# Pooled branch projection as three float32r products, and new rates for spreading the modulation sums

## The chip, the cores and the metric

One core of a Trainium2 chip runs the whole kernel in one launch. The metric is the device time in microseconds (us). The engines are PE (TensorE, matrix products), DVE (VectorE), ACT (ScalarE), POOL (GpSimd) and SP (which issues most DMA transfers). Each has a queue of its own and works through it in order; semaphores tie them together.

## The reference, cut to what matters

One decoder block for 256 tokens of width 2048, all in float32. The vector c gives six modulation rows (ada); the first half of the block mixes tokens by a sparse attention and by a causal pooling, merges both with gates and projects; the second half is a product-key retrieval over 16384 single-neuron experts, which the kernel computes densely.

```python
mod = einsum('bd,de->be', silu(c), w_ada) + b_ada            # 12288 values: sh1, sc1, gt1, sh2, sc2, gt2
h = rms_norm(x, g_norm1) * (1 + sc1) + sh1
q, k, v, iq, ik, iw, pl, ga, gp = split(h @ w_in)
attn = dsa_sparse_attention(...)                              # indexer scores, top 64 keys, softmax
pooled = trailing means of pl over 2/4/8/16 positions, minus pl
pooled = (per-group linear map of pooled) * pool_scale        # 256 tokens x 1024
y_pool = pooled @ w_pool_br                                   # 1024 -> 2048
merged = sigmoid(ga) * (attn @ w_attn_br) + sigmoid(gp) * y_pool
x = x + gt1 * (merged @ w_out)
h = rms_norm(x, g_norm2) * (1 + sc2) + sh2
x = x + gt2 * peer(h)                                         # q @ keys, top 16 x top 16, gelu(h @ u) * gates @ v
```

## The kernel before, in words

Activations lie with the features on the partitions: a tile is 128 features x 256 tokens, and 16 tiles make the width of 2048. Weights stream from HBM in rows of 128 x 2048 values (1 MB) into four buffers named `raw`, issued by SP in the order in which the program asks for them; a buffer is free for the transfer after next but three when its last reader is done.

Most matrix products are made in float32r from split operands. `split` (L121) rounds half a raw row (128 x 1024) into `wH` on ACT (L125) and puts the rest into `wL` on DVE (L126); three buffers of each rotate. `mm3` (L133) then makes three products per weight tile: high weight by high activation (L135), high by low (L136), low by high (L137). The projection of the pooled branch is the exception: there the raw row and the pooled values go into one plain float32 product (L510), which the trace shows as two records each.

The stages in order: three passes over the combined input projection; values and index weights; the pooled branch (`pool_map`, L477, makes the eight pooled tiles `pooled`, then 16 output tiles j of 8 products each, each joined to the pool gate on DVE at L511); the attention gate projection (`wga`, sigmoid at L522); the attention projection (`branch`, L496, with DVE's joins L533, L534 and L537); the output projection (L552); norm and query projection; then the expert tables, the up phase (128 table rows in 256 steps, products L934 and L935) and two down phases.

Beside these stages run two kinds of side work. One is a list of closures (`side`): index scores (L354 to L360), selection of the top keys (L373, L374), norms of q and k (L391 to L401) and attention (L414 to L446); each output tile of the pooled branch runs two of them. The other is the modulation. An ada sum (L140) multiplies a raw row of `w_ada` by silu(c) and adds it up on DVE. 32 of the 96 sums are due before the input projection ends; the other 64 stand in a list `bg`, and `pace(rate)` (L182) adds a rate per output tile to an account and takes one sum from the list for each whole unit. The rates R_K, R_Y, R_GA, R_WO and R_PQ belong to the third input pass, the pooled and the attention projection (both R_Y), the gate projection, the output projection and the query projection. What is left in the list when the up phase is at its sparse part is summed there, one sum before each sparse step (`ada_later`, L838), among tasks that a budget per step doles out; a sparse step gathers 1 MB of expert rows by an indirect DMA and works on them on DVE (L814, L833). The last task ends in a few products (L1005).

Up to the expert tables a scheduler lays out each engine's order from the program; from there on the order is that of the code.

Of the kernel before, what the change touches and what calls it, by code (L numbers as in the profile page):

```python
# [10 lines left out]
F32R = mybir.dt.float32r  # L11
# [3 lines left out]
ALU = mybir.AluOpType  # L15
# [4 lines left out]
P = 128  # L20
T = 256
D = 2048
ND = 16
# [8 lines left out]
KGROUPS = ((0, 4), (4, 10), (10, 16))  # L32
NGU = 43
RAW = 4
R_K, R_Y, R_GA, R_WO, R_PQ = 0.6, 0.75, 0.7, 0.6, 0.3
TB = 8
R_UP, R_D1, R_D2 = 0.97, 0.3, 0.75
KEPT = 9
# [4 lines left out]
def kernel(  # L43
# [25 lines left out]
    dve, act, pe = nc.vector, nc.scalar, nc.tensor  # L69
# [17 lines left out]
    pscale = vecs[:, 194:202]  # L87
# [26 lines left out]
    def load(src, rows=None):  # L114
        raw = stream.tile([P, D], F32, name="raw", bufs=RAW)
        if rows:
            raw = raw.rearrange("p (a b) -> p a b", a=rows)
        nc.sync.dma_start(out=raw, in_=src)
        return raw
# [9 lines left out]
    def load_split(src):  # L129
        raw = load(src)  # L130
        return [split(raw[:, 1024 * i:1024 * i + 1024]) for i in range(2)]

    def mm3(ps, w, off, xH, xL, start, stop, **kw):  # L133
        wH, wL = w[0][:, off:off + P], w[1][:, off:off + P]
        pe.matmul(ps, wH, xH, start=start, stop=False, **kw)  # L135
        pe.matmul(ps, wH, xL, start=False, stop=False, **kw)  # L136
        pe.matmul(ps, wL, xH, start=False, stop=stop, **kw)  # L137
# [34 lines left out]
    def run_side(n):  # L172
        for _ in range(n):
            if side:
                side.pop(0)()
# [6 lines left out]
    def pace(rate):  # L182
        credit[0] += rate
        while credit[0] >= 1.0:
            credit[0] -= 1.0
            if bg:
                ada(bg.pop(0))
# [4 lines left out]
    def small3(i, dtype=F32):  # L192
        return s3.tile([P, T], dtype, name=f"m{i}")
# [10 lines left out]
    def acc_tile():  # L204
        return accp.tile([P, 512], F32, name="acc")

    def misc_tile():
        return misc.tile([P, 512], F32, name="mps")
# [84 lines left out]
    for gi, (ka, kb) in enumerate(KGROUPS):  # L293
# [5 lines left out]
        for r in range(ntiles):  # L299
# [6 lines left out]
            for x, u in enumerate(us):  # L306
                off = x * nb * P
                w = ws[off // step]
                ps = acc_tile()[:, :T]
# [150 lines left out]
    def pool_group(g):  # L460
        w = POOL_WINDOWS[g]
        src = pl[:, 2 * g:2 * g + 2, :]
        cur, step = src, 1
        while step < w:
            nxt = wk.tile([P, 2, T + 16], F32, name="ws", bufs=2)
            dve.tensor_tensor(nxt[:, :, 2 * step - 1:], cur[:, :, 2 * step - 1:],
                              cur[:, :, step - 1:T + 16 - step], ALU.add)
            cur, step = nxt, 2 * step
        pd = wk.tile([P, 2, T], F32, name="pT", bufs=2)
        head = cur[:, :, 16:32]  # L470
        dve.tensor_tensor(head, head, corr[:, g:g + 1, :].to_broadcast([P, 2, 16]), ALU.mult)
        dve.scalar_tensor_tensor(pd, cur[:, :, 16:], 1.0 / w, src[:, :, 16:], op0=ALU.mult, op1=ALU.subtract)
        return pd

    pooled = [None] * ND

    def pool_map(g):  # L477
        pd = pool_group(g)
        if not poolw_box:
            poolw_box.append(load(poolw_in).rearrange("p (g c e) -> p g c e", g=4, c=2))  # L480
        pw = poolw_box[0]
        for e in range(2):
            u = 2 * g + e
            ps = misc_tile()[:, :T]
            for c in range(2):
                pe.matmul(ps, pw[:, g, c, P * e:P * e + P], pd[:, c], start=c == 0, stop=c == 1)
            pooled[u] = small3(u)
            act.mul(pooled[u], ps, pscale[:, u:u + 1])

    for g in range(4):  # L490
        pool_map(g)
        run_side(2)

    ybr = {}

    def branch(b, j, xH, xL):  # L496
        if j % 2 == 0:
            ybr[0] = load_split(ybr_in[b, j // 2])
        ps = acc_tile()[:, :T]
        for k in range(8):  # L500
            mm3(ps, ybr[0][j % 2], k * P, xH[k], xL[k], k == 0, k == 7)
        return ps

    for j in range(ND):
        if j % 2 == 0:
            ybr[0] = load(ybr_in[0, j // 2])
        ps = acc_tile()[:, :T]
        for k in range(8):
            o = 1024 * (j % 2) + P * k
            pe.matmul(ps, ybr[0][:, o:o + P], pooled[k], start=k == 0, stop=k == 7)  # L510
        dve.tensor_tensor(gpool[j], ps, gpool[j], ALU.mult)  # L511
        run_side(2)
        pace(R_Y)

    gattn = [None] * ND
    for j in range(ND):
        ps = acc_tile()[:, :T]
# [12 lines left out]
    for j in range(ND):  # L530
        ps = branch(1, j, [oT[0, k] for k in range(8)], [oT[1, k] for k in range(8)])
# [15 lines left out]
    for j in range(ND):  # L547
        ps = acc_tile()[:, :T]
# [64 lines left out]
    for l in range(2, ND):  # L613
        ps = acc_tile()[:, :T]
# [354 lines left out]
    for k in range(2 * P):  # L969
        e, f = k // 2, k % 2  # L970
        ahead(k)
        if f == 0:
            ps = accp.tile([P, 512], F32, name="acc")
# [43 lines left out]
    for hf in range(2):  # L1017
# [6 lines left out]
        for e in range(P):  # L1024
            k = 2 * P + P * hf + e
# [108 lines left out]
```

## Time and profile before

| | |
|---|---|
| median of 3 runs | 2155.93 us (2154.45 to 2156.39) |
| profiled execution, own time | 2165.35 us |
| its span | 2163.6 us |
| mean granted TensorE clock | 0.982 |
| busy: PE / DVE / ACT / POOL | 96% / 79% / 48% / 7% |
| PE products | 14192 |
| HBM traffic | 595.95 MB read, 42.02 MB written |

The span runs from the first to the last instruction of one profiled execution; its time is measured around it. Busy time is the union of an engine's instructions; PE's records overlap, and their ends are modelled, so distances between starts tell more than durations. PEclk is the granted TensorE clock as a share of full speed: 1.00 is 2.4 GHz, 0.50 is 1.2 GHz.

### The profile page before, as it was taken

The numbers are of one execution on the slowest core, as the hardware profiler recorded it, in microseconds if no ns is written. First come the engines' busy times: TensorE is split into PE (matmuls) and PEld (weight loads), VectorE is DVE, ScalarE is ACT, GpSimd is POOL, SyncE is SP. The second block draws the span as 40 slices with busy tenths as digits, with TensorE's granted clock in tenths as the row PEclk, the third lists the DMA queues.
The fourth block names the chain that finished last, engine by engine and source line by source line (L and its number), as shares of the span: only waits on it lengthen the run. The fifth ranks groups of instructions, "written<-read, shape, count | busy, mean of one in ns | idle before, by whom it ended". The sixth has DMA issues, their size and how long they took to land.

```text
span 2163.6 us, 35340 instructions
## 1 busy us (share of the span) xinstructions
PE 2080.1 (96%) x14192; PEld 1965.9 (91%) x14192; DVE 1704.4 (79%) x2424; ACT 1039.6 (48%) x1405; POOL 142.5 (7%) x120
## 2 busy tenths in 40 slices
PE   6999999999898999999999999989999999999998
PEld 4998997899898999999999999888999998999998
DVE  7888888767877778778887775877777678888855
ACT  4543342463334445555555555444544455544544
POOL 0000000000000000000000000221111012222100
PEclk8999999999899999999999999998999999999999
DMA  9887886768875656676666777999999999999964
GB/s 348 326 314 294 303 307 247 278 242 304 311 291 200 219 212 228 235 262 249 231 231 248 255 279 269 363 399 342 371 361 373 370 374 346 374 375 375 365 221 143
DMA packets 142933, 640.29 MB, mean 296 GB/s; under 512 B 11449, under 2 KB 42193, under 8 KB 94257
## 3 DMA queue, kind: packets, MB, share of 16 engines
q1 hardware_dynamic: 124690, 530.82, 67.5%
q0 software_dynamic: 13472, 92.55, 11.4%
q10 hardware_dynamic: 4608, 14.68, 1.7%
q8 instruction: 111, 1.82, 0.3%
q14 instruction: 52, 0.43, 0.1%
HBM read 595.95 MB, written 42.02 MB: 295 GB/s over the span
## 4 chain that ended last, share of the span: by engine, by line
PE 47%; issue 24%; DMA 13%; DVE 10%; ACT 3%; POOL 1%; SPq 0%; DVEq 0%; ACTq 0%; POOLq 0%
PE acc L934 16%; PE acc L935 8%; DMA raw<-in_ada_dram 6%; PE acc L137 5%; DMA raw<-in_v_dram 5%; PE acc L135 5%; PE acc L136 5%; PE gp L934 4%; DVE raw L140 4%; DVE wL L126 3%; PE gp L935 2%; ACT wH L125 2%; DMA raw<-in_u_dram 1%; PE acc L510 1%; DMA r<-in_urow_dram,idxS 0%
## 5 line engine op out<-in xcount | busy, mean ns | idle before, releaser
L125 ACT CAST wH<-raw 128x1024 fp32r<-128x1024 f32 (+2 forms) x738 | 751.1, 1022 | 926.3 <-PE acc L934 278.5
L126 DVE TENSOR_TENSOR wL<-raw,wH 128x1024 fp32r<-128x1024 f32 (+2 forms) x738 | 871.3, 1188 | 329.1 <-ACT wH L125 326.4
L934 PE MATMUL acc<-hHL,wH 128*128 128x448 f32 x2048 | 655.7, 377 | 0.5 <-ACT r L601 0.5
L935 PE MATMUL acc<-hHL,wL 128*128 128x224 f32 x2048 | 546.8, 267 | 9.3 <-DVE wL L126 9.2
L934 PE MATMUL acc<-aHL,wH 128*128 128x448 f32 x1536 | 503.6, 378 | 7.6 <-DVE ast L961 5.0
L935 PE MATMUL acc<-aHL,wL 128*128 128x224 f32 x1536 | 409.6, 267 | 6.5 <-DVE wL L126 6.2
L934 PEld LDWEIGHTS acc<-hHL,wH 128*128 128x128 f32 x2048 | 386.3, 189 | 29.2 <-ACT r L601 0.7
L935 PEld LDWEIGHTS acc<-hHL,wL 128*128 128x128 f32 x2048 | 393.3, 192 | 12.2 <-DVE wL L126 12.1
L135 PE MATMUL acc<-hHL,wH 128*128 128x256 f32 x1200 | 345.9, 289 | 19.2 <-ACT wH L125 17.9
L137 PE MATMUL acc<-hHL,wL 128*128 128x256 f32 x1200 | 342.0, 287 | 8.7 <-DVE wL L126 8.6
L136 PE MATMUL acc<-hHL,wH 128*128 128x256 f32 x1200 | 342.1, 286 | 0.1
L934 PEld LDWEIGHTS acc<-aHL,wH 128*128 128x128 f32 x1536 | 290.8, 189 | 29.8 <-DVE ast L961 5.3
L935 PEld LDWEIGHTS acc<-aHL,wL 128*128 128x128 f32 x1536 | 296.2, 193 | 12.2 <-DVE wL L126 12.1
L135 PEld LDWEIGHTS acc<-hHL,wH 128*128 128x128 f32 x1200 | 232.4, 194 | 23.9 <-ACT wH L125 21.4
L140 DVE CUSTOM_DVE_ANT_0 raw<-raw,cb 128x2048 f32<-128x2048 f32 x96 | 219.7, 2288 | 43.4 <-DMA raw<-in_ada_dram 37.6
L137 PEld LDWEIGHTS acc<-hHL,wL 128*128 128x128 f32 x1200 | 231.5, 194 | 11.8 <-DVE wL L126 11.5
L136 PEld LDWEIGHTS acc<-hHL,wH 128*128 128x128 f32 x1200 | 232.5, 194 | 0.8 <-DVE hHL L574 0.3
L934 PE MATMUL gp<-aHL,wH 128*128 128x448 f32 x512 | 177.1, 377 | 0.4 <-DVE xT L998 0.4
L935 PE MATMUL gp<-aHL,wL 128*128 128x224 f32 x512 | 135.4, 264 | 0.0
L934 PEld LDWEIGHTS gp<-aHL,wH 128*128 128x128 f32 x512 | 96.4, 188 | 8.0 <-DVE xT L998 1.0
L935 PEld LDWEIGHTS gp<-aHL,wL 128*128 128x128 f32 x512 | 98.2, 192 | 0.0
L814 DVE CUSTOM_DVE_ANT_0 r<-r,hs 128x2048 f32<-128x2048 f32 x32 | 73.2, 2287 | 15.1 <-DMA r<-in_urow_dram,idxS 15.1
(250 smaller groups left out, 2070.5 us busy)
## 6 DMA issues: line engine op xcount, KB each, us to landing
raw<-in_u_dram SPq DMA_DIRECT2D x128, 1024.0 KB, 5.1
raw<-in_v_dram SPq DMA_DIRECT2D x128, 1024.0 KB, 9.5
raw<-in_ada_dram SPq DMA_DIRECT2D x96, 1024.0 KB, 5.7
raw<-in_wgrp_dram SPq DMA_DIRECT2D x43, 768.0 KB, 6.0
ab<-adram SPq DMA_DIRECT2D x55, 448.0 KB, 8.8
raw<-in_ybr_dram SPq DMA_DIRECT2D x16, 1024.0 KB, 6.6
raw<-in_wga_dram SPq DMA_DIRECT2D x16, 1024.0 KB, 4.8
raw<-in_wout_dram SPq DMA_DIRECT2D x16, 1024.0 KB, 5.0
```

The costliest lines, as they stand in the source:

```text
L125: act.copy(wH[:, :n], src)
L126: dve.tensor_tensor(wL[:, :n], src, wH[:, :n], ALU.subtract)
L135: pe.matmul(ps, wH, xH, start=start, stop=False, **kw)
L136: pe.matmul(ps, wH, xL, start=False, stop=False, **kw)
L137: pe.matmul(ps, wL, xH, start=False, stop=stop, **kw)
L140: dve.tensor_tensor_reduce(raw, raw, cb, scale=1.0, scalar=0.0, op0=ALU.mult, op1=ALU.add, accum_out=modr[:, i:i + 1])
L510: pe.matmul(ps, ybr[0][:, o:o + P], pooled[k], start=k == 0, stop=k == 7)
L814: dve.tensor_tensor_reduce(rows, rows, made["h"], scale=1.0, scalar=0.0, op0=ALU.mult, op1=ALU.add, accum_out=aS[:, n:n + 1])
L934: pe.matmul(ps[:, :2 * N].rearrange("p (a n) -> p a n", a=2), wH, xHL, start=start, stop=False)
L935: pe.matmul(ps[:, :N], wL, xHL[:, 0], start=False, stop=stop)
```

## The change

The pooled values are kept in two halves. ACT writes the scaled result of the linear map as float32r, and DVE writes what the rounding left (a new instruction, `scalar_tensor_tensor`, eight in all) into tiles m8 to m15. The projection then calls `branch`, as the attention projection does: each raw row is split in two by ACT and DVE, and each weight tile is used in three float32r products, 384 in place of 128 float32 ones. The rates of the ada sums change beside it: R_Y from 0.75 to 0.45, R_GA from 0.7 to 0.8, R_PQ from 0.3 to 0.4.

```diff
-R_K, R_Y, R_GA, R_WO, R_PQ = 0.6, 0.75, 0.7, 0.6, 0.3
+R_K, R_Y, R_GA, R_WO, R_PQ = 0.6, 0.45, 0.8, 0.6, 0.4
...
-    pooled = [None] * ND
+    pooled = [[None] * 8, [None] * 8]
...
-            pooled[u] = small3(u)
-            act.mul(pooled[u], ps, pscale[:, u:u + 1])
+            pooled[0][u], pooled[1][u] = small3(u, F32R), small3(8 + u, F32R)
+            act.mul(pooled[0][u], ps, pscale[:, u:u + 1])
+            dve.scalar_tensor_tensor(pooled[1][u], ps, pscale[:, u:u + 1], pooled[0][u], op0=ALU.mult, op1=ALU.subtract)
...
     for j in range(ND):
-        if j % 2 == 0:
-            ybr[0] = load(ybr_in[0, j // 2])
-        ps = acc_tile()[:, :T]
-        for k in range(8):
-            o = 1024 * (j % 2) + P * k
-            pe.matmul(ps, ybr[0][:, o:o + P], pooled[k], start=k == 0, stop=k == 7)
+        ps = branch(0, j, pooled[0], pooled[1])
         dve.tensor_tensor(gpool[j], ps, gpool[j], ALU.mult)
```

From the second edit on lines move up by 1 to 4: L511 of before is L507 after, L533 is L529, L814 is L810.

DVE in the pooled stage, where the selection of keys ends (L378 and L380 are its last steps; r1 with acc is the join of an output tile, raw with modr an ada sum). Before:

```order
L380 TENSOR_TENSOR sc1_3545<-sc1_3545,addmask_75 128x128
L140 ISA raw_4006,modr_96<-raw_4006,cb_66 128x2048
L140 ISA modr_96 128x1
L511 TENSOR_TENSOR r1_253<-acc_3905,r1_253 128x256
L511 TENSOR_TENSOR r1_253<-acc_3932,r1_253 128x256
L140 ISA raw_4027,modr_96<-raw_4027,cb_66 128x2048
L140 ISA modr_96 128x1
L511 TENSOR_TENSOR r1_253<-acc_3952,r1_253 128x256
```

And after, at the same place:

```order
L380 TENSOR_TENSOR sc1_3545<-sc1_3545,addmask_75 128x128
L507 TENSOR_TENSOR r1_253<-acc_4107,r1_253 128x256
L394 TENSOR_SCALAR relu_4203<-mps_4172 10x256
L126 TENSOR_TENSOR wL_4219<-raw_4216,wH_4218 128x1024
L126 TENSOR_TENSOR wL_4223<-raw_4216,wH_4222 128x1024
L507 TENSOR_TENSOR r1_253<-acc_4146,r1_253 128x256
L151 RECIPROCAL rs_y_4204<-sg_4205 10x256
L140 ISA raw_4258,modr_96<-raw_4258,cb_66 128x2048
```

Where two ada sums stood between joins, two splits of a weight row stand now, and one sum follows. Over the whole stage the order has 13 ada sums before and 7 after, and 16 more splits of the projection's weights.

DVE in the attention projection, tiles 7 and 8 (sg with acc is the join L533, L529 after). Before:

```order
L533 TENSOR_TENSOR sg_5705<-acc_5680,m7_4898 128x256
L126 TENSOR_TENSOR wL_5717<-raw_5714,wH_5716 128x1024
L537 TENSOR_TENSOR m6_5674<-sg_5671,pl_5406 128x256
L534 TENSOR_TENSOR sg_5705<-sg_5705,r1_253 128x256
L126 TENSOR_TENSOR wL_5721<-raw_5714,wH_5720 128x1024
L537 TENSOR_TENSOR m7_5708<-sg_5705,pl_5406 128x256
L140 ISA raw_5755,modr_96<-raw_5755,cb_66 128x2048
L140 ISA modr_96 128x1
L533 TENSOR_TENSOR sg_5749<-acc_5724,m8_4959 128x256
```

And after:

```order
L529 TENSOR_TENSOR sg_6026<-acc_6001,m7_5219 128x256
L126 TENSOR_TENSOR wL_6039<-raw_6032,wH_6038 128x1024
L533 TENSOR_TENSOR m6_5995<-sg_5992,pl_5733 128x256
L530 TENSOR_TENSOR sg_6026<-sg_6026,r1_253 128x256
L126 TENSOR_TENSOR wL_6110<-raw_6107,wH_6109 128x1024
L529 TENSOR_TENSOR sg_6067<-acc_6042,m8_5283 128x256
```

The ada sum that stood in front of the join of tile 8 is gone from there. From the first to the last of these joins the order has 10 sums before and 6 after.

DVE in the sparse part of the up phase (r1 with aS is a sparse step, ast the join of an up tile). After the second sparse step stood, before:

```order
L147 TENSOR_TENSOR mod_97<-modr_96,vecs_69 128x16
L814 ISA r1_14327,aS_8332<-r1_14327,hs_13991 128x2048
```

And after:

```order
L957 TENSOR_TENSOR ast_14724<-acc_14825,join_14870 128x224
L126 TENSOR_TENSOR wL_14891<-raw_14767,wH_14890 128x1024
L140 ISA raw_14862,modr_96<-raw_14862,cb_66 128x2048
L140 ISA modr_96 128x1
L126 TENSOR_TENSOR wL_14914<-raw_14816,wH_14913 128x1024
L957 TENSOR_TENSOR ast_14919<-acc_14873,join_14920 128x224
L810 ISA r1_14642,aS_8647<-r1_14642,hs_14306 128x2048
```

Before, the modulation was complete here (L147 adds its last bias) and sparse steps followed one another; now an ada sum stands before each of nine sparse steps, where two had one. 12 sparse steps come before the last up tile, where 19 did.

## Rows read from the trace of the kernel before

**Rows 1.** Busy time of each engine in stretches: us, PE, PEld, DVE, ACT, POOL, PEclk, DMA, GB/s.

```profile
321.90:355.40 33.50, 33.50 (x178) 25.62 (x177) 26.68 (x52) 13.84 (x44) 0.00 (x0) 1.00 0.65 226
355.40:372.50 17.10, 17.10 (x81) 15.08 (x80) 17.07 (x65) 0.14 (x1) 0.00 (x0) 1.00 0.60 223
372.50:410.70 38.20, 36.57 (x151) 26.81 (x150) 29.03 (x51) 9.54 (x17) 0.00 (x0) 0.91 0.76 287
...
410.70:522.00 111.30, 109.08 (x873) 107.39 (x872) 76.34 (x131) 70.22 (x128) 0.00 (x0) 0.98 0.72 270
522.00:582.00 60.00, 50.27 (x368) 48.98 (x368) 57.12 (x85) 22.31 (x32) 0.00 (x0) 0.89 0.89 318
582.00:684.00 102.00, 99.58 (x794) 98.01 (x792) 75.36 (x94) 40.35 (x49) 0.00 (x0) 0.98 0.74 269
...
1356.00:1486.00 130.00, 121.40 (x733) 113.29 (x732) 108.40 (x115) 58.97 (x76) 30.66 (x20) 0.96 0.98 375
...
1820.00:2054.00 234.00, 232.76 (x1481) 221.57 (x1479) 202.25 (x162) 119.97 (x124) 46.44 (x27) 1.00 0.97 370
```

**Rows 2.** Groups of instructions over the span: count, busy us, mean ns, idle before.

```profile
L126 DVE TENSOR_TENSOR wL<-raw,wH 128x1024 fp32r<-128x1024 f32 x645 | 784.2, 1222 | 320.4 <-ACT wH L125 317.9
L125 ACT CAST wH<-raw 128x1024 fp32r<-128x1024 f32 x645 | 674.7, 1050 | 819.6 <-PE acc L934 278.5 <-PE gp L934 260.5 <-PE acc L136 149.3
...
L135 PEld LDWEIGHTS acc<-hHL,wH 128*128 128x128 f32 x1200 | 232.4, 194 | 23.9 <-ACT wH L125 21.4 <-ACT hHL L573 1.5 <-issue 0.6
L140 DVE CUSTOM_DVE_ANT_0 raw<-raw,cb 128x2048 f32<-128x2048 f32 x96 | 219.7, 2288 | 43.4 <-DMA raw<-in_ada_dram 37.6 <-ACT n L211 5.6
...
L360 DVE SCALAR_TENSOR_TENSOR sc<-relu,iw,sc 128x256 f32<-128x256 f32 x15 | 7.2, 482 | 1.4 <-ACT relu L356 1.2
```

**Rows 3.** PE in order of time: start, us, instruction, count, idle before.

```profile
363.79 9.44 PE L510 MATMUL acc<-m,raw 128*128 128x256 f32 x43
...
388.11 2.42 PE L400 MATMUL mps<-rs_y,ident 10*128 10x256 f32 x10 [1.63 <-DVE rs_y L155]
...
410.27 0.28 PE L135 MATMUL acc<-hHL,wH 128*128 128x256 f32 x1
...
411.94 0.28 PE L137 MATMUL acc<-hHL,wL 128*128 128x256 f32 x1
```

**Rows 4.** DVE in order of time: two splits in a row.

```profile
401.93 2.35 DVE L126 TENSOR_TENSOR wL<-raw,wH 128x1024 fp32r<-128x1024 f32 x2
```

**Rows 5.** Groups of instructions, DVE, 321.9 to 410.7 us: the ada sums.

```profile
L140 DVE CUSTOM_DVE_ANT_0 raw<-raw,cb 128x2048 f32<-128x2048 f32 x13 | 29.7, 2288 | 9.7 <-DMA raw<-in_ada_dram 9.7
```

**Rows 6.** DVE in order of time: first and last attention join, first output join.

```profile
524.23 0.42 DVE L533 TENSOR_TENSOR sg<-acc,m 128x256 f32<-128x256 f32 x1
...
578.96 0.42 DVE L533 TENSOR_TENSOR sg<-acc,m 128x256 f32<-128x256 f32 x1
...
588.81 0.48 DVE L552 SCALAR_TENSOR_TENSOR xT<-acc,mod,xT 128x256 f32<-128x256 f32 x1 [0.99 <-PE acc L137]
```

**Rows 7.** Who waited for whom, 522 to 582 us: total us, times, longest.

```profile
PE acc L137 <- DVE wL L126: 8.7, 4, 3.2
...
DVE sg L533 <- PE acc L137: 2.9, 3, 1.1
```

**Rows 8.** Busy times, columns as in rows 1, of two short stretches.

```profile
579.30:586.10 6.80, 5.53 (x26) 5.53 (x27) 6.71 (x9) 2.12 (x4) 0.00 (x0) 0.50 0.85 325
391.60:398.40 6.80, 6.80 (x16) 4.50 (x16) 5.81 (x7) 0.00 (x0) 0.00 (x0) 0.50 0.69 263
```

**Rows 9.** Who waited for whom, 1356 to 1486 us.

```profile
PE acc L935 <- DVE wL L126: 8.4, 7, 3.2
ACT wH L125 <- DMA raw<-in_u_dram: 7.6, 2, 5.4
...
DVE raw L140 <- DMA raw<-in_ada_dram: 1.1, 1, 1.1
```

**Rows 10.** The last products of the task list: count, duration ns, first and last start.

```profile
L1005 PE MATMUL acc<-selS,hs x24: 202/276/277, 2060.7 to 2063.6; 128*128 128x32 f32 x24
```

## The prediction, made blind

> **What bounds the kernel now.** I read the profile page first: PE is busy 96% of the span and DVE 79%, averages that say little about one stage. Then the busy times by stage [rows 1], each against its own length, in which the reader is to look for the engine without idle time. From 410.7 to 522 us (the gate projection) PE works 109.1 of 111.3 us: PE is the bound. In the pooled stage (321.9 to 410.7) it changes: in the middle part DVE works 17.07 of 17.10 us, in the first 26.7 of 33.5 and in the last 29.0 of 38.2, where PE works 36.6. From 522 to 582 (attention projection) DVE works 57.1 of 60 and PE 50.3: DVE is the bound, and the list of waits agrees, PE having lost 8.7 us to the low halves that DVE writes [rows 7]. From 1356 to 1486 (the tail of the up phase) the DMA share is 0.98 at 375 GB/s and PE works 121.4 of 130. So the two edits touch three kinds of stage. Third view: the groups of instructions, for prices [rows 2]. Last: the order of time [rows 3, 4, 6], for distances from start to start, since instructions overlap and a duration is longer than what it costs in a row.
>
> **Part 1: three float32r products for one float32.** The 128 old products leave 256 records; 43 of them in a row take 9.44 us, 0.219 us each, so 0.439 us a product [rows 3]. The new form runs right behind: from the first L135 at 410.27 to the L137 at 411.94 there are 14 steps, 0.119 us each [rows 3], so 0.358 us for three. PE saves 128 x 0.081 = 10.4 us of the pooled stage.
>
> A weight load lasts 194 ns [rows 2] and still the products follow each other in 119 ns, so in this trace it is hidden. The Trainium skill (TensorE: Matmul & The Clock Gate, Weight-path perf modes) says that the fast weight load is not for FP32, which would speak against three loads for one product: at 194 ns each they would cost 0.58 us, 18 us more than before. The rows decide against that reading, and the sum goes by 0.119.
>
> DVE pays. Added are 16 splits (two back to back take 2.35 us [rows 4], 1.17 each, 18.8 us) and 8 subtractions that make the low half of the pooled values; the trace has none, the nearest row is L360, the same kind of operation on the same shape, 0.48 us [rows 2], so 3.9 us at most. Taken from this stretch are 6 of its 13 ada sums [rows 5] at 2.30 us (13.8) and 2 of 3 splits of the gate weights (2.3), by the order. Net +6.6 us of DVE work (its parts in rows 1 sum to 72.8 in 88.8 us). ACT gets 16 casts of 1.05 us [rows 2] on 23.5 us of work [rows 1], and has the room.
>
> Which ends last differs by part. First part (DVE 26.7 of 33.5): +6 splits (a seventh falls before it), +8 subtractions, -1 ada sum = 7.0 + 3.9 - 2.3 = +8.6. Of its 6.8 us of idle time much was waiting for ada rows (9.7 us in the stage [rows 5]); I let 3 of it stay, so it ends 4.8 us later. Middle part (DVE full): 3 splits in, 2 ada sums out, 3.5 - 4.6 = -1.1. Last part (PE 36.6 of 38.2): seven tiles of eight products save 56 x 0.081 = 4.5; DVE there, 29.0 + 6 splits - 2 gate splits - 3 ada sums = 26.8, fits in. Sum 4.8 - 1.1 - 4.5 = **-0.8 us**. Bounds: -8 if DVE's idle time takes all splits, +6 if none of it does.
>
> **Part 2: the ada rates.** Of 64 sums that are spread, the order has these places before and after: pooled stage 13 and 7, attention projection 10 and 6 (first to last L533), tail of the up phase 2 and 9; the others move by one or two in stages where PE is the bound (DVE 76 of 111 and 75 of 102 us [rows 1]) and are hidden there; without that cover each would cost 2.3 us.
>
> Attention projection. First to last L533 is 54.7 us for 15 tiles [rows 6]; DVE idled only 2.9 of it [rows 7]. Without 4 sums DVE needs 54.7 - 2.9 - 9.2 = 42.6 us; PE needs 15 x 24 x 0.119 = 42.8. Two engines so alike wait for each other; by the share that DVE reaches here now (57.1 of 60, 0.95) 42.8 becomes 45.1, and I add 2.4 for lost clock (PEclk 0.89 over 60 us [rows 1] is 6.6 now): 47.5, **-7 us**. Bounds: -11 (PE's own time plus 1) and -2 (as full of waits as now: three quarters of what DVE loses given back).
>
> Next stage's start. From the last L533 to the first L552 are 9.85 us [rows 6], while its 48 products need 5.7. The granted clock was 0.50 from 579.3 to 586.1 [rows 8], right behind the waits for low halves. If PE waits less, half of those 3.4 us come back: **-2** (0 to -4).
>
> Tail of the up phase. Seven more ada rows of 1 MB are loaded and summed between the gathered rows, and seven gathers move behind it: as many bytes in the same DMA-bound stretch. What changes is whose buffers they take: ada rows share the four raw buffers with the weights, and have a step or two to land. Before, one of two ada sums waited 1.1 us, and two weight loads 7.6 us [rows 9]; the gathers' waits shrink in turn. I take **+1**; bounds -4 and +21 (the rival below). The task list then ends 7 x 2.37 of work later, at 0.75 a block 22 blocks or some 55 us after 2060.7 [rows 10], with PE at 232.8 of 234 us under the same gathers [rows 1], and 2163 still ahead: 0.
>
> Sum: -0.8 - 7 - 2 + 1 = -8.8 us. The profiled execution took 2165.35 us (span 2163.6 and 1.75 around it), so it becomes 2156.55; the median of the runs shown is 2155.93, 0.99565 of the profiled time, and so the prediction is **2147.2 us**.
>
> **Rivals.**
> Full gain: PE follows everywhere, pooled stage -8, attention -11, clock -3, tail 0: -22, 2134 us. For it: DVE's idle time in the pooled stage is mostly waiting for ada rows. Against: PE needs low halves in order, behind long DVE work.
> Gain spent in the pooled stage: the splits queue on DVE behind index and selection work, PE starves in the first two parts and the granted clock falls, as from 391.6 to 398.4 after PE had waited 1.63 us for L155 [rows 3, 8]. A stretch of 6.8 us at half speed costs 3.4; two more are +6.8, the stage then +6; attention, as tight, gives -5, the next stage's clock nothing, the tail +1: +2, 2158 us, no change. The skill's section on HAM oscillation in the same page names gaps between groups of matmuls as what brings the clock down; it speaks for this rival, and the trace agrees at this one place.
> Slower: in the tail each ada sum waits for its row, and DVE, in order, holds the splits and the joins behind it, and PE after them. Two late weight loads, 7.6 us, stand beside 8.4 us of PE waiting for low halves [rows 9], so a wait passes on nearly whole. Seven sums late by 3 us (the longest wait for a raw load was 5.4) cost 21 in place of the 1: +11, 2167 us. It decides from 9.8 / 7 = 1.4 us a sum, where it has eaten the other terms. Against: the one measured wait is 1.1, and the gathers that they replace waited too.
> That the change does not happen is no case: the order shows both edits.
>
> **Numbers.** Forecast 0.50, full gain 0.15, spent in the pooled stage 0.21, slower 0.14. A difference under 0.2% (4.3 us) counts as no change, about what a measurement of this kernel can tell. Faster: 0.15 and nearly all of the forecast, 0.64; same 0.21; slower 0.15. The forecast's own range is 2141 to 2153; to leave out no more than 2 in 10 it reaches to the better half of the full gain and most of the slower case: 2132 to 2164.
>
> **What would show it.** Right: L507's products at 0.119 us, the pooled stage at 87 us with DVE above 78 us of work in it; first to last of the attention joins (L529) at 47 to 48 us; PE's wait for low halves there under 5 us; the up tail within 3 us of 130. Wrong: a pooled stage of 92 us or more with more half-speed stretches; ada waits above 10 us in the tail; or attention joins still 52 us apart.

## The result and the profile after

The changed kernel takes 2147.07 us (median of 22 runs, 2139.85 to 2157.07) against 2158.35 us before (22 runs beside them, 2150.8 to 2166.72). The ratio is 0.9947 with a 95% interval of 0.9933 to 0.9961, so about 11 us faster. The forecast was 2147.2 us, 8.8 below the 2155.93 of three runs before; that the time itself was met to 0.1 us is in part luck, since the kernel before came out 2.4 us higher over 22 runs. Several terms of the sum did not come out: in front of the up phase the gain was larger than forecast, behind it the loss was. The profiled execution of the changed kernel is the slowest of its 22 (2157.07 us, span 2155.3). Executions of one kernel spread over some 17 us here, so a stage read from one profile carries part of that spread; below, lengths of stages are compared over several profiled executions where that decides something.

Distances, all from starts to starts of the same instructions (last value product, last pooled join, last sigmoid of the attention gate, last attention join, first product of the up phase, its last product, last product of the second down phase). The two middle columns are the first two experiments:

| us | before | split only | rates only | both (after) |
|---|---|---|---|---|
| pooled stage | 88.7 | 91.4 | 89.4 | 82.2 |
| gate projection | 109.4 | 109.3 | 106.4 | 107.4 |
| attention projection | 59.0 | 55.7 | 47.1 | 49.3 |
| up to the start of the up phase | 214.6 | 213.0 | 209.8 | 209.7 |
| these four | 471.7 | 469.4 | 452.7 | 448.6 |
| up phase | 692.3 | 691.1 | 698.1 | 699.0 |
| down phases | 671.9 | 674.2 | 678.6 | 680.2 |
| all | 1835.9 | 1834.7 | 1829.4 | 1827.8 |
| lost at half clock in these four | 17.1 | 17.1 | 8.5 | 6.8 |
| in the up phase | 5.1 | 1.7 | 6.8 | 6.8 |
| in the down phases | 6.8 | 6.8 | 10.2 | 11.9 |

The last three rows are half the length of the pieces in which the granted clock was 0.50. A length less this loss is called the length at equal clock below; it is exact where PE alone sets the pace, and takes off too much where something else does.

In front of the up phase the change gains 23.1 us, far more than the 9.8 of the prediction's first terms. Behind it 15.0 are given back, where 1 was priced. Of the 23.1 us, 10.2 are less time lost at half clock; of the 15.0, 6.8 are more of it.

Busy times of the kernel after in stretches (the three parts of the pooled stage, the gate and the attention projection, the tail of the up phase; columns as in [rows 1]):

```profile
321.60:358.20 36.60, 36.49 (x251) 29.96 (x250) 34.75 (x65) 20.59 (x51) 0.00 (x0) 1.00 0.58 211
358.20:372.75 14.55, 13.23 (x90) 9.85 (x89) 14.55 (x59) 4.71 (x9) 0.00 (x0) 1.00 0.45 150
372.75:403.90 31.15, 30.29 (x195) 26.94 (x194) 27.12 (x50) 11.49 (x15) 0.00 (x0) 0.89 0.64 227
...
403.80:511.20 107.40, 106.53 (x861) 104.87 (x860) 83.53 (x141) 71.14 (x128) 0.00 (x0) 1.00 0.79 291
511.20:560.50 49.30, 46.33 (x382) 45.75 (x381) 45.62 (x72) 21.86 (x32) 0.00 (x0) 1.00 0.85 296
...
1333.90:1469.20 135.30, 120.78 (x723) 112.79 (x723) 105.38 (x113) 58.03 (x74) 19.58 (x13) 0.95 0.95 354
```

Against [rows 1]: the first part of the pooled stage is 3.1 us longer, with DVE now at 34.75 of 36.6; the middle part, where DVE has no idle time in either kernel, is 2.6 shorter; the last is 7.1 shorter. In the tail PE does the same 121 us of work in more time (135.3 us in place of 130.0), and the rate falls from 375 to 354 GB/s: about the same bytes take longer, so something is waited for.

The groups of DVE instructions in the pooled stage show the added work and what became of the ada sums [rows 5] (count | busy us, mean ns | idle before):

```profile
L126 DVE TENSOR_TENSOR wL<-raw,wH 128x1024 fp32r<-128x1024 f32 x16 | 19.2, 1214 | 0.0
L140 DVE CUSTOM_DVE_ANT_0 raw<-raw,cb 128x2048 f32<-128x2048 f32 x7 | 15.9, 2278 | 1.2 <-DMA raw<-in_ada_dram 1.1
...
L489 DVE SCALAR_TENSOR_TENSOR m<-mps,vecs,m 128x256 fp32r<-128x256 f32 x8 | 3.8, 481 | 1.1 <-ACT m L488 1.0
```

16 splits cost 19.2 us and the eight new subtractions 3.8, both as priced (18.8 and at most 3.9); the wait for ada rows fell from 9.7 to 1.1 us.

PE in order of time, at half and at full clock, inside the new projection (start, us, instruction):

```profile
388.03 0.41 PE L137 MATMUL acc<-m,wL 128*128 128x256 f32 x1
388.25 0.41 PE L135 MATMUL acc<-m,wH 128*128 128x256 f32 x1
...
393.09 0.28 PE L137 MATMUL acc<-m,wL 128*128 128x256 f32 x1
393.21 0.28 PE L135 MATMUL acc<-m,wH 128*128 128x256 f32 x1
```

A product follows the last by 0.12 us at full clock (0.22 at half), so three cost 0.36 us as priced from [rows 3].

In the attention projection PE hardly waits for low halves any more, against 8.7 us in [rows 7]:

```profile
DVE sg L529 <- PE acc L137: 0.7, 1, 0.7
PE acc L137 <- DVE wL L126: 0.6, 1, 0.6
```

The tail of the up phase is where the loss starts. Who waited for whom in it (total us, times, longest), beside [rows 9]:

```profile
PE acc L931 <- DVE wL L126: 14.3, 6, 5.5
DVE raw L140 <- DMA raw<-in_ada_dram: 11.9, 4, 5.0
ACT wH L125 <- DMA raw<-in_u_dram: 6.9, 4, 1.8
```

One of these waits followed through, first on DVE, then on PE, each in order of time (in brackets the idle time before, and who ended it):

```profile
1365.46 0.38 DVE L957 TENSOR_TENSOR ast<-acc,join 128x224 f32<-128x224 f32 x1
1370.83 2.29 DVE L140 CUSTOM_DVE_ANT_0 raw<-raw,cb 128x2048 f32<-128x2048 f32 x1 [4.99 <-DMA raw<-in_ada_dram]
1373.05 0.08 DVE L140 DVE_READ_ACCUMULATOR2_ANT modr<- 128x1 f32 x1
1373.05 2.29 DVE L810 CUSTOM_DVE_ANT_0 r<-r,hs 128x2048 f32<-128x2048 f32 x1
1375.26 0.08 DVE L810 DVE_READ_ACCUMULATOR2_ANT aS<- 128x1 f32 x1
1375.26 2.36 DVE L126 TENSOR_TENSOR wL<-raw,wH 128x1024 fp32r<-128x1024 f32 x2
```

```profile
1376.54 0.56 PE L931 MATMUL acc<-hHL,wL 128*128 128x224 f32 x1 [5.51 <-DVE wL L126]
```

DVE stands 5 us for an ada row, then does the sum and the sparse step, and the split that PE needs stands behind both: PE idles 5.51 us. That is the mechanism of the prediction's slower rival. Something follows that the prediction's term for the tail does not have. The granted clock falls inside this wait and stays at 0.50 for 6.8 us:

```profile
1374.60:1381.40 6.80, 4.86 (x17) 4.52 (x17) 4.45 (x6) 0.35 (x1) 1.68 (x1) 0.50 0.89 341
```

The other two half-clock pieces in this tail (from 1408.8 and 1425.8 us) begin within 1 us behind PE's waits of 3.30 and 3.12 us for low halves, and the two of before (from 1412.2 and 1459.9) behind or in waits of 2.02 and 3.22. So a late row seems to cost twice, the wait and the clock behind it; that the wait brings the clock down was not tested by a run of its own.

### The profile page after: what moved, and what is told of

It reads as the page before. It is cut to its first block, busy times and chain, and to the rows that moved or that the text cites. A ratio compares the mean times of both kernels' runs of the same rounds, so it can differ in the third digit from the quotient of the medians.

```text
span 2155.3 us, 35665 instructions
## 1 busy us (share of the span) xinstructions
PE 2067.5 (96%) x14320; PEld 1958.4 (91%) x14320; DVE 1720.8 (80%) x2448; ACT 1057.7 (49%) x1421; POOL 136.1 (6%) x120
## 5 line engine op out<-in xcount | busy, mean ns | idle before, releaser
L125 ACT CAST wH<-raw 128x1024 fp32r<-128x1024 f32 (+2 forms) x754 | 768.8, 1023 | 953.0 <-PE acc L930 283.7
L126 DVE TENSOR_TENSOR wL<-raw,wH 128x1024 fp32r<-128x1024 f32 (+2 forms) x754 | 889.2, 1187 | 315.3 <-ACT wH L125 310.7
L135 PE MATMUL acc<-hHL,wH 128*128 128x256 f32 x1200 | 344.6, 288 | 20.5 <-ACT wH L125 18.1
L137 PE MATMUL acc<-hHL,wL 128*128 128x256 f32 x1200 | 340.6, 286 | 8.2 <-DVE wL L126 7.9
L135 PEld LDWEIGHTS acc<-hHL,wH 128*128 128x128 f32 x1200 | 231.2, 193 | 25.2 <-ACT wH L125 23.1
L137 PEld LDWEIGHTS acc<-hHL,wL 128*128 128x128 f32 x1200 | 230.3, 193 | 10.8 <-DVE wL L126 10.6
L136 PE MATMUL acc<-m,wH 128*128 128x256 f32 x384 | 108.9, 284 | 0.0
```

The lines of the kernel that those rows point to most:

```text
L125: act.copy(wH[:, :n], src)
L126: dve.tensor_tensor(wL[:, :n], src, wH[:, :n], ALU.subtract)
```

## The experiments

Medians and ratios are against the kernel before on the same chip.

**Split only** (the changed kernel with the old rates) and **rates only** (the kernel before with the new ones).

```diff
-R_K, R_Y, R_GA, R_WO, R_PQ = 0.6, 0.45, 0.8, 0.6, 0.4
+R_K, R_Y, R_GA, R_WO, R_PQ = 0.6, 0.75, 0.7, 0.6, 0.3
```

> The kernel after with the old ada rates (0.75, 0.7, 0.3 for R_Y, R_GA, R_PQ): the split products alone. Theory A (the gain of the pooled stage needs both edits, because DVE has to give up ada sums to make room for the low halves): DVE work in the pooled stage rises from 72.8 to about 95 us, so the stage grows from 88.8 to 94 to 97 us, the attention joins stay about 54 us apart, the tail of the up phase stays about 130 us, and the time is 2158 to 2166 us, not below before. Theory B (the cheaper products carry the gain and the rates only shift work): pooled stage 82 to 84 us as in the kernel after, time about 2150 us.

> The kernel before with the new ada rates (0.45, 0.8, 0.4): the rates alone, plain float32 products. Theory A (moved sums free DVE in front and cost the tail): attention joins 47 to 48 us apart, pooled stage 85 to 87 us, the up phase starts 12 to 16 us earlier than before, the tail of the up phase takes 135 to 137 us with 8 to 12 us of DVE waits for ada rows, and the time is 2152 to 2160 us: about nothing is left. Theory B (the tail's loss in the kernel after is no consequence of the moved sums): tail about 130 us, time about 2144 us.

Split only: 2161.9 us, ratio 1.0007 [0.9991, 1.0023], no change. Rates only: 2151.69 us, 0.9967 [0.9948, 0.9986], a small gain where theory A (2152 to 2160 us) left about none. For the split alone the time is theory A's, but the length of the pooled stage lies in neither theory's window (94 to 97, 82 to 84):

```profile
321.50:412.90 91.40, 85.10 (x529) 70.92 (x527) 82.63 (x177) 34.90 (x71) 0.00 (x0) 0.91 0.61 224
```

The order had put only 11 ada sums there, so DVE has 82.6 us of work and not 95, and the stage is 91.4 (the attention joins are 51.8 apart, where 54 was expected). PE waits 6.3 us in it for low halves, against 1.6 in the changed kernel, so DVE's sums do stand in PE's way; but 8.5 us of the 91.4 are lost at half clock, where before had 3.4. At equal clock the stage is 82.9 us against 85.3: the split alone is worth some 2 us there. The rates alone leave the pooled stage at 89.4 with PE busy 87.98 of it; they shorten the attention projection by 11.9, so that the up phase starts 19 us earlier after the last value product (12 to 16 expected, with part of it in the pooled stage), and they bring 12.5 of the 15.0 us that are lost behind the up phase's start (up phase 698.1, down 678.6). Its waits in the tail are those of the kernel after, though no product there is new:

```profile
PE acc L935 <- DVE wL L126: 14.7, 7, 6.5
DVE raw L140 <- DMA raw<-in_ada_dram: 12.2, 4, 6.3
```

So the loss comes for the most part with the moved sums, theory A, and the gain in front needs both edits only in the pooled stage.

**Seven or eight sums back out of the tail**: R_GA 1.25 for 0.8 puts them into the gate projection (two are left in the tail), R_PQ 0.95 for 0.4 into the query projection (one is left).

> The kernel after with R_GA 1.25 in place of 0.8: about 7 more ada sums in the gate projection, where PE is the bound, so that the tail of the up phase has 1 or 2 sums again, as before. Theory A (the moved sums cost the tail and the down phases): front as in the kernel after (up phase starts within 4 us of 770), tail back to about 130 us with under 2 us of ada waits, time 2131 to 2139 us. Theory B (the loss behind the up phase's start has another cause, such as the different time at which the whole tail runs): tail 135 us or more, time about 2147 us. Theory C (seven more sums fill DVE in the gate projection, 84.7 + 16.1 = 101 of 109 us, and PE waits there): tail about 130 us, but the gate projection 6 us or more longer, time 2142 to 2147 us.

> The kernel after with R_PQ 0.95 in place of 0.4: about 7 more ada sums in the query projection in place of the tail of the up phase. Theory A: tail about 130 us, DVE in the query projection 75 + 16 = 91 of 102 us hidden under PE, time 2131 to 2139 us, the same as with the sums in the gate projection. Theory B: no better than after, 2147 us, tail 135 us or more. Theory C (the query projection has no room: its DVE work stands in a few dense pieces): the up phase starts 6 us or more later than in the kernel after, and the time is 2140 to 2147 us.

2141.81 us, 0.9912 [0.9888, 0.9936], and 2141.64 us, 0.9911 [0.9889, 0.9933]: both below the changed kernel, and both some 2.7 us above the window that theory A gave. The up phase is back at 692.8 and 691.5 us, the down phases at 674.1 in both, so theory B falls. Where the sums go is not quite free: in the gate projection DVE comes to 97 us and the stage grows from 107.4 to 113.3 (close to theory C's 6 us); with the sums in the query projection the way from the last attention join to the up phase grows by 1.0 us.

```profile
398.40:511.70 113.30, 108.42 (x854) 105.78 (x854) 96.98 (x154) 70.46 (x127) 0.00 (x0) 0.98 0.90 334
```

**The sum later, the load where it was**: four pauses of the task list in place of two between an ada row's load and its sum.

```diff
         raw = load(ada_in[i])
-        yield None
-        yield None
+        for _ in range(4):
+            yield None
         ada_sum(raw, i)
```

> The kernel after, but each ada row in the tail of the up phase gets four pauses of the task list in place of two between the issue of its load and its sum, so that it has about twice the time to land. From the first sparse step to the last up product: 128.4 us before (2 sums), 135.1 in the kernel after (9 sums). Theory A (the tail's loss is DVE waiting in order for rows that land late): DVE's waits for ada rows fall from 11.9 us to under 3, the stretch takes 128 to 131 us, the time is about 2142 us. Theory B (the rows' bytes and their hold on the four raw buffers cost, not the place of the sum): the waits for ada rows fall but others rise (weight rows held up), the stretch stays at 134 us or more and the time at about 2147 us or above.

2132.71 us, 0.9874 [0.9846, 0.9903]. The nine sums are all still in the tail, with the same bytes, and the up phase takes 690.3 us in place of 699.0 (the stretch named in the expectation 121.7, below the window of theory A, and the time is 9 us below the 2142 that it gave). DVE waits for no ada row, and PE's wait is down to 5.2:

```profile
ACT wH L125 <- DMA raw<-in_u_dram: 17.3, 5, 8.4
PEld acc L931 <- DVE wL L126: 8.3, 10, 1.5
PE acc L931 <- DVE wL L126: 5.2, 8, 1.2
```

Theory A holds: with the same bytes, held longer, the loss in the up phase is gone, so it is the time at which DVE comes to the sum. (Weight rows are waited for more, 17.3 us, so theory B's cost exists, but is smaller.) With the longer pause the first sparse step starts 5 us later, which is why the whole up phase is compared. Not foreseen: the down phases fall to 663.0, 17 us below the changed kernel, and make most of this kernel's gain.

**The load without the sum.** This kernel leaves the nine sums out and sets their table to zero at the start.

> The kernel after without the sums of the tail: the nine rows are loaded there in the same places and nothing reads them, so that the modulation sums in question are left at zero; the task list's budget counts them as before. Theory A (DVE's part: waiting for the row and 2.3 us of work each): the stretch from the first sparse step to the last up product falls from 135.1 to 127 to 130 us. Theory B (bytes in a DMA-bound stretch, nine times 1 MB at 370 GB/s): it stays at 133 to 136 us.

One execution, 2147.49 us. The stretch took 133.3 us, in theory B's window. The waits for ada rows are gone, and ACT now waits for weight rows instead, 44.6 us against 6.9 in the changed kernel.

```profile
ACT wH L126 <- DMA raw<-in_u_dram: 44.6, 11, 7.3
```

Taking the reader away changed when the rows and buffers come round, so this run took away more than the sum; how, was not followed. By itself it speaks for theory B. The run before weighs more, since it keeps every load and every sum and moves only the time of the sum; but that loads without a reader cost as much stays unexplained.

**The plain products with the good rates** (R_PQ 0.95), and **no ada sums at the pooled tiles** (split, `pace(R_Y)` taken out there, R_WO 1.0, R_PQ 0.95).

> The kernel before (plain float32 products) with the rates of the kernel that had 0.95 in the query projection: what the split products are worth once the rates are good. Theory A (the pooled stage needs both edits: PE bounds it with plain products, DVE with 13 sums): pooled stage (last value product to last pooled join) 88 to 90 us against 79.3 with split products, time 8 to 10 us above the split kernel with these rates, some 2150 us. Theory B (the rates do it all; the split gain is lost in later waits): time within 3 us of 2141.6.

> The kernel after with no ada sums taken at the pooled branch's tiles, R_WO 1.0 and R_PQ 0.95, so that the seven sums move to the output and query projections, where DVE has room. Theory A (DVE bounds the pooled stage with split products, at 2.3 us a sum): the pooled stage falls from 79.3 to 66 to 73 us and the time to 2126 to 2136 us. Theory B (with the splits in, the selection's chain or PE bounds it): pooled stage 77 to 80 us, time 2139 to 2143 us. Theory C (the output projection has no room for the sums): first to last of its joins grows from 91.8 us to 96 or more.

2139.76 us, 0.9908 [0.9885, 0.9932]: by time theory B, no difference from the split kernel with these rates (2141.64), although the pooled stage is 86.6 us against 79.3, close to theory A's 88 to 90. And 2140.37 us, 0.9907 [0.9884, 0.993], theory B: two sums still run in the pooled stage where seven did (from 386.9 and 398.2 us), and it is 79.3 again, at equal clock 75.9 against 77.6. So at seven sums DVE hardly bounds it any more; PE works 78.6 of the 79.3 us.

```profile
321.30:400.60 79.30, 78.57 (x538) 66.84 (x537) 68.03 (x165) 37.77 (x74) 0.00 (x0) 0.96 0.41 140
```

**Pauses again, with and without the split, and with three.** Four pauses with plain products; three pauses with split; four pauses with R_PQ 0.95, split and plain.

> The kernel before (plain float32 products) with the rates of the change and four pauses in place of two between an ada load and its sum in the tail: the partner of the run with the same pauses and split products (2132.7 us). Theory A (the split is worth what its stage shows, 6 to 7 us, once nothing else moves): pooled stage 86 to 90 us, time 2138 to 2141 us. Theory B (what the pooled stage gains is lost again further on): time 2130 to 2136 us. On the down phases: theory P (the pauses shift the sparse steps against the weight rows, whatever stands in front): from the first product of the first down phase to the last product 652 to 657 us, with under 25 us of ACT waiting for rows of v up to the last sparse product of the up table; theory Q (it was one lucky execution): 664 to 670 us and 60 us or more.

> The kernel after with three pauses in place of two. Theory A (the sum waits because its row lands late): waits for ada rows between those with two (11.9 us) and with four pauses (none), under 4 us, and first sparse step to last up product 123 to 131 us. Theory P (the down phases follow from the place of the sparse steps in a block): they may fall on either side, 654 or 668 us, but ACT's waits for rows of v go with them (about 16 or about 74 us). Time 2133 to 2143 us.

> The kernel after with R_PQ 0.95 and four pauses: both remedies. Theory A (the remedies mend the same loss: seven sums gone from the tail, or no wait for them): no better than with the pauses alone in the tail, 124 to 128 us; the time is 2130 to 2140 us, by whether the down phases fall at 654 or 664 us. Theory B (they add): time under 2128 us.

> The same as the run with R_PQ 0.95 and four pauses, with plain float32 products in the pooled branch. Theory A (the split is worth 6 to 7 us): 6 to 8 us above that run. Theory B (its gain is lost further on): within 3 us of it. Together with the other three pairs (rates of before, rates of the change, R_PQ 0.95) this gives the worth of the split products at five settings of the rest.

2135.54 us, 0.9888 [0.986, 0.9915]; 2137.08, 0.9914 [0.9882, 0.9945]; **2125.15, 0.9846 [0.9818, 0.9874]**; 2129.86, 0.9875 [0.9843, 0.9906]. The third beats both kernels, the one before by 33 us. By their windows of time the first and the third fall to theory B; the second lies in the one window that it had; the fourth, 4.7 us above the third, lies between A and B.

The tail over the profiles of all kernels that make every sum, by sums left for it and pauses. "Lost" is what half clock took of the column before it. ACT's waits are those for rows of v, from the first product into the tile gp, some 10 us into the first down phase, to the last sparse step on the up table; with nine sums this stretch is some 110 us longer, so they compare within a pair.

| sums, pauses | up phase | lost | DVE waits for ada rows | down phases | lost | ACT waits for v |
|---|---|---|---|---|---|---|
| 2, two (before) | 692.3 | 5.1 | 1.1 | 671.9 | 6.8 | 51.1 |
| 2, two (split only) | 691.1 | 1.7 | 1.3 | 674.2 | 6.8 | 52.2 |
| 2, two (split, R_GA 1.25) | 692.8 | 5.1 | 1.4 | 674.1 | 6.8 | 56.4 |
| 2, two (no sums at the pooled tiles) | 688.7 | 3.4 | 1.5 | 676.2 | 6.8 | 55.1 |
| 1, two (split, R_PQ 0.95) | 691.5 | 1.7 | 0 | 674.1 | 6.8 | 39.6 |
| 1, two (plain, R_PQ 0.95) | 687.8 | 0 | 0 | 671.1 | 5.1 | 51.4 |
| 9, two (after) | 699.0 | 6.8 | 11.9 | 680.2 | 11.9 | 73.9 |
| 9, two (plain) | 698.1 | 6.8 | 12.2 | 678.6 | 10.2 | 64.1 |
| 9, three (split) | 694.6 | 1.7 | 4.5 | 665.7 | 8.5 | 7.3 |
| 9, four (split) | 690.3 | 3.4 | 0 | 663.0 | 8.5 | 15.8 |
| 9, four (plain) | 690.9 | 3.4 | 0 | 669.5 | 13.7 | 29.9 |
| 1, four (split) | 689.7 | 0 | 0 | 660.4 | 5.1 | 13.0 |
| 1, four (plain) | 688.7 | 3.4 | 0 | 662.1 | 6.8 | 24.6 |

By length the up phase follows the ada waits, with three pauses between two and four (4.5 us of wait, where under 4 was expected): theory A. Taking the sums away and letting them land mend the same 8 us there. About half of the 8 is clock. At equal clock the up phase is 692.1 and 691.2 us with nine sums and two pauses, 685.3 to 689.8 with two sums or one, 686.9 and 687.4 with nine and four pauses, but 692.8 with three pauses, where PE still waits 12.5 us for low halves in the tail. So the step at three pauses is not shown at equal clock.

The down phases show theory P: with four pauses they are 9 to 17 us shorter than their partners with two, in all four pairs that differ in nothing else, even where only one sum is left, and ACT's waits for v go with them. At equal clock all four pairs gain 11 to 14 us, from 665.9 to 668.4 down to 654.5 to 655.9. Two profiles of kernels that differ in the pauses alone (R_PQ 0.95, split; two pauses, then four) show it, of the same stretch:

```profile
ACT wH L125 <- DMA raw<-in_v_dram: 39.6, 15, 4.3
...
PE acc L931 <- DVE wL L126: 3.9, 12, 0.7
```

```profile
ACT wH L125 <- DMA raw<-in_v_dram: 13.0, 8, 2.4
```

With four pauses no wait of PE for low halves is left in that list. The pauses shift where in a block a sparse step stands; which alignment of gathered rows, written gates and rows of v makes the difference was not tried, and stays open. The plain kernel with nine sums (down 669.5 in all, 659.5 from the first product into gp, 29.9 us of waits) fell between the numbers of P and Q, nearer to P; it also lost the most at half clock, 13.7 us, and without them stands at 655.9 as the other three do.

What the split itself is worth, from five pairs that differ only in it (ratio split minus ratio plain, half-widths put together as root of squares): old rates +0.07% ± 0.16; new rates -0.20 ± 0.24; R_PQ 0.95 +0.03 ± 0.33; four pauses -0.14 ± 0.40; both -0.29 ± 0.42. The last four, weighted by their widths, give -0.15% ± 0.16, or 3 us with 0 to 7 open. None is resolved by itself, and whether the two remedies add (0.9846 against 0.9874) is not either. In the four pairs of profiles with new rates the whole way from the last value product to the last down product is 1.6, 1.7, 7.0 and 3.6 us shorter with the split at equal clock, on the average half of the 7 us that the pooled stage alone is worth (next section); the gate projection takes 0.3 to 1.3 us longer in each, and where the rest goes was not followed.

## Why the prediction was right, and where it was not

**Right by its own steps.** The price of the products, the splits and the subtractions. The attention projection: 47.3 us from first to last join where 47.5 was forecast, with PE's waits for low halves at 0.6; rates only gave 45.0, so this term belongs to the rates. (The new products stand at L135 to L137; L507, which the prediction names for them, is their join.)

**Pooled stage: -0.8 forecast, -6.5 measured.** The mechanism was right (first part longer, last shorter), its sizes were not. The first part got 3.1 us longer and not 4.8, since the wait for ada rows fell from 9.7 to 1.1 us where 3 was left standing; the middle was 2.6 shorter against 1.1, the last 7.1 against 4.5. The term was sized with the clock of one execution, and the clock of this stage varies: 0.88 to 0.98 in the seven split kernels that have the order of the changed one here, for stages of 79.3 to 87.0 us. At equal clock the stage is 84.3 to 85.3 us in the five plain kernels, 76.8 to 78.7 in these seven, 82.9 with the split and the old rates. So the worth at equal clock is 7 us, most of PE's 10.4, and it needs the sums out of the way. Two of the prediction's own signs for this stage, 87 us and more than 78 us of DVE work, were not met (82.2 and 76.3).

The rival that spends the gain at half clock does happen, in two of these seven. In the fastest kernel the stage ran so:

```profile
320.60:407.60 87.00, 85.33 (x529) 71.38 (x528) 76.09 (x171) 36.22 (x74) 0.00 (x0) 0.88 0.55 197
383.10:403.60 20.50, 20.50 (x77) 17.12 (x75) 12.38 (x21) 2.98 (x3) 0.00 (x0) 0.50 0.47 162
```

20.5 us at half clock cost 10.2. In order of time, what stands ahead of the drop:

```profile
380.11 0.38 PE L135 MATMUL acc<-m,wH 128*128 128x256 f32 x1 [0.54 <-ACT wH L125]
...
380.93 0.38 PE L137 MATMUL acc<-m,wL 128*128 128x256 f32 x1 [0.32 <-DVE wL L126]
...
381.48 3.07 PE L400 MATMUL mps<-rs_y,ident 10*128 10x256 f32 x10
384.48 0.58 PE L137 MATMUL acc<-m,wL 128*128 128x256 f32 x1
```

Two waits of 0.54 and 0.32 us, and ten products of ten output rows, among which the granted clock falls (at 383.1); from 384.48 on the records are those of half clock. The Trainium skill (TensorE: Matmul & The Clock Gate, HAM oscillation) blames gaps between groups of matmuls. The trace agrees as to the place, but the gaps here sum to 0.86 us, so they were not shown to be the cause; the narrow products stand there as well.

**Next stage's start: -2 forecast, -4.0 measured** (9.8 to 5.8 us from the last attention join to the first output join). All of the half-speed stretch went, not half of it: the granted clock is 1.00 there.

```profile
560.50:568.00 7.50, 7.50 (x65) 7.50 (x64) 7.50 (x12) 3.24 (x5) 0.00 (x0) 1.00 0.77 268
```

**Gate projection: 0 forecast, -2.0**, for the most part a half-speed stretch of before that did not come again (1.7 us lost there, none after). What else was not counted in front, 3.2 us, lies between the last sigmoid and the first attention join (4.3 to 2.0 us) and behind the first output join (0.9).

**Tail: +1 forecast, +6.7 measured.** This is the step that failed: "a step or two to land" was taken to be enough because the one measured wait was 1.1 us. With nine sums between gathers four rows came late, 11.9 us in all, above the 10 that the prediction had named as a sign of being wrong. It cost 6.7 / 7 = 0.96 us a sum, and the up phase as a whole 8 us between nine sums and one or two (means of 698.6 over two profiles and 690.7 over six, all with two pauses), of which 4 are half-clock time (6.8 us lost against 2.9). The rival had the mechanism and a price of 3 us; its own point of decision, 1.4 us a sum, was not reached. Neither it nor the forecast counted the clock in the tail.

**Down phases: 0 forecast, +8.3 in this pair**, 5.8 between the means of the same profiles (679.4 and 673.6). The prediction let the later end of the task list cost nothing, "with PE at 232.8 of 234 us under the same gathers [rows 1], and 2163 still ahead: 0". The tasks do end 45 us later (55 were worked out):

```profile
L1001 PE MATMUL acc<-selS,hs x24: 203/276/402, 2105.5 to 2108.5; 128*128 128x32 f32 x24
```

But most of what the phases lost is clock. 11.9 us went to half clock against 6.8 before, in two pieces: from 1473.6 us, at the start of the first down phase, and from 2108.5, with the last of the products above. At equal clock the growth is 3.2 us in this pair, 667.0 to 668.3 between the means, and 1.1, 2.5, -0.8 and 0.6 us in the four pairs that differ only in whether the seven or eight sums stay in the tail. So the 0 was near the mark at equal clock. All five kernels with nine sums lose 8.5 to 13.7 us to half clock here, all eight with two or one 5.1 to 6.8, so the loss does come with the moved sums; why these pieces get longer with them was not followed.

So the time was met because 13 us of gain too little were counted in front and 14 us of loss too little behind: two errors that cancelled. The step that failed by its mechanism is the tail's; much of the rest is granted clock, which the forecast took over from one execution.

## What to carry to other kernels

Work that is moved off a compute-bound stage into a DMA-bound one has to be priced at the queue it waits in: an in-order engine that waits for a late row holds everything behind it, and the cure is to leave the load where it is and take the use later, or to put the work where its engine has room and the DMA too. Cheaper products help only where PE ends last, and the engine that pays for them must first be cleared. Compare a stage over several executions at equal clock before its length is explained: the down phases here seemed to lose 8 us to the moved work, and most of it was time at half clock.

## What was not expected of the hardware

With the same instructions in the same order, the pooled stage ran from 79.3 to 87.0 us, nearly all of it by the granted clock (76.8 to 78.7 at equal clock). The part ahead of it varied too: the last value product started between 316.8 and 321.6 us in kernels that are the same up to there. And two more pauses in a task list shortened the down phases by up to 17 us, 11 to 14 at equal clock, with the same bytes moved.
